# Norms of a two-layer trunk: the reciprocal root by a bit pattern and Newton steps on GpSimd in place of ScalarE's square root

## The chip, the cores and the metric

The kernel runs on one core of a Trainium2 chip. The metric is device time in microseconds (us) of one execution. Before the change three runs gave a median of 1860.58 us (1860.45 to 1862.76). The engines are named as in the profile: PE is TensorE (PEld its weight loads), DVE is VectorE, ACT is ScalarE, POOL is GpSimd, SP is SyncE, which issues most of the transfers.

## The reference, cut to what matters

A trunk of two layers on 512 tokens of width 1024. Each layer has a SwiGLU part, a mixer and another SwiGLU part, each behind a root-mean-square norm; a last norm follows. The mixer has eight forgetting-attention heads and four differential heads, whose outputs are normed once more, head by head ("norm of the diff heads").

```python
def _rmsnorm(x, gain):
    y = x32 * lax.rsqrt(jnp.mean(x32 * x32, axis=-1, keepdims=True) + NORM_EPS)
    return (y * gain).astype(x.dtype)
...
x = x + 1/2 * SwiGLU_1(RMSNorm(x))
x = x + W_out [FoX_heads(h) ; Diff_heads(h)],  h = RMSNorm(x)
x = x + 1/2 * SwiGLU_2(RMSNorm(x))
...
lam = exp(sum(lq1 * lk1)) - exp(sum(lq2 * lk2)) + lambda_init
o_d = _rmsnorm(o_d, subln) * (1.0 - lambda_init)
```

## The kernel before, in words

The tokens lie in four blocks of 128 (tiles `xs`), and every float32 operand of a large product is split in two parts, a rounded high part and the rest (low part), so that a product is three matmuls. For the mixer `prep_plain` turns a pair of 128-wide slices of x (k pair `kp`) with TensorE into a PSUM bank, scales it by the norm's gain and writes the operand tile `XA<kp>`: the high half by ScalarE (`act.activation`), the low half by VectorE (`scalar_tensor_tensor`). The root of the norm is not in these operands. It is applied to the results: the projections that follow (`proj`) start on the raw operands, and the root comes in as a row of 512 factors.

That row is made so. `half_squares` sums the squares on ScalarE into `s2`; `rms` adds the two halves (VectorE), scales, takes the square root on ScalarE, the reciprocal on VectorE, one Newton step (`refine`, four VectorE instructions) and the negative. All of it lies in the small tile `nst`, 128 partitions by 4 values. `diag` multiplies the unit matrix by the root of each of the four blocks (`dg`: two blocks on VectorE, two on ScalarE), and `finish_norm` multiplies `dg` by ones on TensorE, which spreads the row over the partitions; ScalarE copies it out as `rb`, and the rope tables are scaled by it. `finish_norm` is called in the middle of the second half of the first projection. It also makes `exl`, the two exponentials of the lambda, from `ls`.

The mixer's order of units is: first projection, then the values of the diff heads, then the rest of the projections between the heads' softmax. A head's softmax is a reduction on VectorE (`ISA` in the trace), exp on ScalarE, a reciprocal on VectorE and a scaling; TensorE turns the probabilities, ScalarE and VectorE split them (`pair`), and TensorE multiplies them with the values (`vd`, `vf`). When the last diff head is through, `stats` starts `diff_norm`: four rows of mean squares (`vv`) go by SP to HBM and come back as a tile `nd` of 64 partitions by 32 values; square root, reciprocal and `refine` follow, and the roots go by SP to HBM (`ms_d`) and come back spread over the partitions, one tile `rbd` for each head. VectorE multiplies each head with it (`ou`), and ScalarE and VectorE split the product (`y`) for the output projection.

ScalarE keeps its functions in tables. Where a square root stands between other functions, an `ACT_TABLE_LOAD` stands ahead of it and another ahead of the next exp or silu.

Each engine works its instructions off in one fixed queue. The order in these queues is set when the kernel is built, by a scheduler that estimates when each instruction can start; code that is written later may so stand earlier in a queue. `tc.issue_after(norm["root"].ins)` is a constraint on that scheduler: the exp of the lambda may not be queued ahead of the norm's square root.

Of the kernel before, what the change touches and what calls it, by code (L numbers as in the profile page):

```python
# [8 lines left out]
F32 = mybir.dt.float32  # L9
F32R = mybir.dt.float32r  # L10
BF16 = mybir.dt.bfloat16
AF = mybir.ActivationFunctionType
ALU = mybir.AluOpType
AX = mybir.AxisListType
# [38 lines left out]
def trunk(ctx, tc, xT, x, gains, gain_row, w_gu, w_dn, w_in, w_ff, w_out, fbias, lams, subln, consts, rope, out):  # L53
# [238 lines left out]
    def refine(y, v, t):  # L292
# [3 lines left out]
        dve.tensor_scalar(out=t, in0=t, scalar1=-0.5, scalar2=1.5, op0=ALU.mult, op1=ALU.add)  # L296
        dve.tensor_tensor(out=y, in0=y, in1=t, op=ALU.mult)

    norm = {}

    def squares(half):
# [13 lines left out]
            act.activation(out=sq, in_=xs[t][:, c * S:(c + 1) * S], func=AF.Square,  # L315
                           accum_out=norm["s2"][:, c, t:t + 1])

    def rms(ss=None):

        st = sm.tile([P, 4, NB], F32, tag="nst", name="nst", bufs=2)  # L320
        v, t, rc, nr = [st[:, i] for i in range(4)]
        if "s2" in norm:
            s2, ss = norm.pop("s2"), v
            dve.tensor_tensor(out=v, in0=s2[:, 0], in1=s2[:, 1], op=ALU.add)
        dve.tensor_scalar(out=v, in0=norm.pop("ss") if ss is None else ss, scalar1=1.0 / D, scalar2=EPS,
                          op0=ALU.mult, op1=ALU.add)
        norm["root"] = act.activation(out=rc, in_=v, func=AF.Sqrt)
        dve.reciprocal(out=rc, in_=rc)
        refine(rc, v, t)
        dve.tensor_scalar(out=nr, in0=rc, scalar1=-1.0, scalar2=None, op0=ALU.mult)  # L330
        norm["rc"], norm["nr"] = rc, nr

    def turn_x(half, kp, tag=None):
# [261 lines left out]
    def mixer(l, n_next, mid):  # L595
# [48 lines left out]
        def finish_norm():  # L644
            p = psum("b")
            pe.matmul(p, rf(ones), nrm.pop("dg"), start=True, stop=True)
            rb = nrm["rb"] = bb[0]
            act.copy(out=rb, in_=p)
            for i in range(2):
                dve.tensor_tensor(out=rope_t[i], in0=rope_t[i], in1=rb, op=ALU.mult)  # L650
            exl = sm.tile([P, 2], F32, tag="exl", name="exl", bufs=1)

            with tc.issue_after(norm["root"].ins):
                act.activation(out=exl, in_=ls, func=AF.Exp)
            dve.tensor_scalar(out=nlam, in0=exl[:, 1:2], scalar1=exl[:, 0:1], scalar2=-lam_init,
                              op0=ALU.subtract, op1=ALU.add)

# [306 lines left out]
        def diff_norm():  # L964

            v_d = dram.tile([DIFF_H, S], F32, name="v_d")
            ms_d = dram.tile([DIFF_H, S], F32, name="ms_d")
            for h in range(DIFF_H):
                sp.dma_start(out=v_d[h:h + 1, :], in_=vv[32 * h:32 * h + 1, :])
            nd = t_tile([64, 3, 32], F32, "nd")  # L970
            v, y, t = nd[:, 0], nd[:, 1], nd[:, 2]
            sp.dma_start(out=v, in_=v_d.rearrange("h (a b) -> (h a) b", b=32))
            act.activation(out=y, in_=v, func=AF.Sqrt)
            dve.reciprocal(out=y, in_=y)
            refine(y, v, t)
            sp.dma_start(out=ms_d.rearrange("h (a b) -> (h a) b", b=32), in_=y)

            def one(h):
                rbd = t_tile([P, S], F32, "rbd")
                sp.dma_start(out=rbd, in_=ms_d[h:h + 1, :].partition_broadcast(P))  # L980
                u = t_tile([P, S], F32, "ou")
                dve.scalar_tensor_tensor(out=u, in0=ov[h], scalar=sub_s, in1=rbd, op0=ALU.mult, op1=ALU.mult)
                split_o(4 + h, u)
            for h in range(DIFF_H):
                later.append(lambda h=h: one(h))
# [226 lines left out]
        for kp in (2, 3):  # L1212
            prep(1, kp, held.pop(0))

    def sums():
        half_squares((0, 1), 1)
        rms()


    xf = home("y0", [P, KP, 2, S], F32, "xin")  # L1220
# [111 lines left out]
    for l in range(DEPTH):  # L1332
# [6 lines left out]

        def mid():  # L1340
            rest_of(plain_)
            sums()
        mixer(l, n + 1, mid)
        pieces = {0: [lambda: [forms_(1, kp, None) for kp in (0, 1)]],
                  1: [lambda: [forms_(1, kp, None) for kp in (2, 3)], lambda: squares(1), rms]}
# [100 lines left out]
```

## Time and profile before

| | |
|---|---|
| median of 3 runs | 1860.58 us (1860.45 to 1862.76) |
| profiled execution | 1860.16 us, of which the span of the trace is 1858.2 us |
| granted TensorE clock | 0.998 |
| PE busy | 1829.4 us, 98% |
| VectorE busy | 1610.3 us, 87% |
| ScalarE busy | 1137.7 us, 61% |
| GpSimd busy | 128.2 us, 7%, in 154 instructions |
| bytes | 303.81 MB, mean 164 GB/s |

The span runs from the first to the last recorded instruction. In a row of a timeline the first number is the start, the second the duration, both in us; then engine, line, operation, and tiles as out<-in; in brackets stands the idle time ahead of it on its engine and what ended it. The mixer of layer 0 begins at about 350 us, that of layer 1 at about 1268 us.

### The profile page before, as it was taken

How to read it: one execution, taken by the hardware profiler on the slowest of the kernel's cores; microseconds unless marked ns; L12 is line 12 of the kernel's file. 1: busy time of each engine (PE TensorE's matmuls, PEld its weight loads, DVE VectorE, ACT ScalarE, POOL GpSimd, SP SyncE). 2: the span in 40 equal slices, each digit the busy share in tenths (PEclk: the TensorE clock that was granted, in tenths of full speed). 3: DMA queues.
4: the chain of work that ended last, by engine and by line, in shares of the span. 5: the costliest groups of instructions: out<-in, count | busy, mean ns of one | idle time of the engine just before them, and what ended most of it. 6: DMA issues, size and time to landing. Idle time of an engine off the chain costs nothing.

```text
span 1858.2 us, 24541 instructions
## 1 busy us (share of the span) xinstructions
PE 1829.4 (98%) x8702; PEld 1492.4 (80%) x8702; DVE 1610.3 (87%) x2531; ACT 1137.7 (61%) x1819; POOL 128.2 (7%) x154
## 2 busy tenths in 40 slices
PE   9999999999999999999999999999999999999997
PEld 5888888777878889888878988887777788888885
DVE  7898899888686999898998989997787869898998
ACT  7555555557795755565575556545677957455564
POOL 2010000000000100100000000000000000000101
PEclk9999999999999999999999999999999999999999
DMA  9786655243336775777557667543333467756742
GB/s 313 206 229 185 188 141 153 91 125 112 105 115 170 204 204 149 197 204 201 139 167 211 171 160 212 157 128 108 110 112 109 134 167 193 224 132 192 216 116 88
DMA packets 95531, 303.81 MB, mean 164 GB/s; under 512 B 12568, under 2 KB 15128, under 8 KB 95408
## 3 DMA queue, kind: packets, MB, share of 16 engines
q1 hardware_dynamic: 74816, 232.15, 36.9%
q0 software_dynamic: 19296, 68.17, 20.7%
q10 hardware_dynamic: 1296, 1.93, 0.3%
q8 instruction: 68, 1.11, 0.2%
q14 instruction: 55, 0.45, 0.1%
HBM read 287.45 MB, written 2.16 MB: 156 GB/s over the span
## 4 chain that ended last, share of the span: by engine, by line
PE 85%; DVE 8%; ACT 3%; DMA 2%; issue 1%; SPq 0%; DVEq 0%; ACTq 0%
PE ps_c L401 12%; PE ps_c L403 12%; PE ps_c L402 12%; PE ps L403 9%; PE ps L402 9%; PE ps L401 9%; PE ps_a L402 4%; PE ps_a L401 4%; PE ps_a L403 3%; DVE wg L84 2%; PE ps_t L497 2%; DVE x L526 1%; PE ps_g L1265 1%; PE ps_b L888 1%; PE ps_b L838 1%; PE ps_b L839 1%
## 5 line engine op out<-in xcount | busy, mean ns | idle before, releaser
L83 ACT CAST wg<-raw 128x1024 fp32r<-128x1024 f32 (+1 forms) x525 | 537.9, 1032 | 480.8 <-PE ps_c L403 173.0
L84 DVE TENSOR_TENSOR wg<-raw,wg 128x1024 fp32r<-128x1024 f32 (+1 forms) x525 | 621.2, 1194 | 101.1 <-ACT wg L83 96.5
L401 PE MATMUL ps_c<-wg,xf 128*128 128x512 f32 (+1 forms) x736 | 277.7, 378 | 1.7 <-ACT wg L83 1.6
L402 PE MATMUL ps_c<-wg,xf 128*128 128x512 f32 (+1 forms) x736 | 276.5, 376 | 1.4 <-DVE wg L84 1.4
L403 PE MATMUL ps_c<-wg,xf 128*128 128x512 f32 (+1 forms) x736 | 275.7, 375 | 0.0
L401 PE MATMUL ps<-wg,xf 128*128 128x512 f32 (+1 forms) x552 | 210.1, 381 | 0.0
L402 PE MATMUL ps<-wg,xf 128*128 128x512 f32 (+1 forms) x552 | 207.3, 376 | 0.9 <-DVE wg L84 0.9
L403 PE MATMUL ps<-wg,xf 128*128 128x512 f32 (+1 forms) x552 | 206.7, 376 | 0.0
L401 PEld LDWEIGHTS ps_c<-wg,xf 128*128 128x128 f32 x736 | 138.3, 188 | 28.6 <-ACT wg L83 2.5
L402 PEld LDWEIGHTS ps_c<-wg,xf 128*128 128x128 f32 x736 | 138.5, 188 | 27.2 <-DVE wg L84 2.2
L403 PEld LDWEIGHTS ps_c<-wg,xf 128*128 128x128 f32 x736 | 138.5, 188 | 25.0
L134 POOL DMA_DIRECT2D raw<-w_gu x86 | 74.6, 867 | 1129.7 <-DMA raw<-w_gu 628.0
L401 PE MATMUL ps_c<-wg,hf 128*128 128x512 f32 x352 | 138.5, 393 | 4.2 <-DVE x L526 4.0
L402 PE MATMUL ps_c<-wg,hf 128*128 128x512 f32 x352 | 137.4, 390 | 0.0
L403 PE MATMUL ps_c<-wg,hf 128*128 128x512 f32 x352 | 137.1, 390 | 0.0
L526 DVE SCALAR_TENSOR_TENSOR x<-ps_c,x 128x512 f32<-128x512 f32 x192 | 124.8, 687 | 1.3 <-PE ps_c L403 1.2
L402 PEld LDWEIGHTS ps<-wg,xf 128*128 128x128 f32 x552 | 104.0, 188 | 18.9 <-DVE wg L84 1.3
L403 PEld LDWEIGHTS ps<-wg,xf 128*128 128x128 f32 x552 | 103.8, 188 | 18.9
L401 PEld LDWEIGHTS ps<-wg,xf 128*128 128x128 f32 x552 | 104.0, 188 | 17.9 <-ACT xf L83 0.4
L401 PE MATMUL ps_a<-XA,wg 128*128 128x512 f32 x256 | 105.8, 414 | 2.2 <-ACT XA L355 1.8
L402 PE MATMUL ps<-wg,hf 128*128 128x512 f32 x264 | 103.1, 391 | 0.0
L401 PE MATMUL ps<-wg,hf 128*128 128x512 f32 x264 | 103.1, 390 | 0.0
(290 smaller groups left out, 3550.9 us busy)
## 6 DMA issues: line engine op xcount, KB each, us to landing
raw<-w_gu SPq DMA_DIRECT2D x218, 512.0 KB, 4.7
raw<-w_dn SPq DMA_DIRECT2D x100, 512.0 KB, 4.4
raw<-w_gu POOLq DMA_DIRECT2D x86, 512.0 KB, 6.8
raw<-w_in SPq DMA_DIRECT2D x48, 512.0 KB, 3.3
raw<-w_dn POOLq DMA_DIRECT2D x40, 512.0 KB, 5.9
kdup<-qk_t SPq DMA_DIRECT2D x64, 128.0 KB, 2.3
raw<-w_out SPq DMA_DIRECT2D x16, 512.0 KB, 3.2
raw<-w_dn SPq DMA_DIRECT2D x20, 256.0 KB, 3.8
```

The source lines that it names most:

```text
L83: act.copy(out=hi, in_=src)
L84: dve.tensor_tensor(out=lo, in0=src, in1=rf(hi), op=ALU.subtract)
L134: pool.dma_start(out=t, in_=where(two, h)[1], accum_op=ALU.add)
L401: pe.matmul(p, lh, rh, start=start, stop=False, skip_group_check=again)
L402: pe.matmul(p, lh, rl, start=False, stop=False, skip_group_check=again)
L403: pe.matmul(p, ll, rh, start=False, stop=stop, skip_group_check=again)
L497: pe.transpose(pj[j][:, e * 256 + p * P:e * 256 + (p + 1) * P], hs[j][p][:, o:o + P], ident)
L526: dve.scalar_tensor_tensor(out=xc, in0=src, scalar=scale, in1=xc, op0=ALU.mult, op1=ALU.add)
L838: pe.matmul(p[:, 0:w], lq, kk[m][:, 0, 0:w], start=True, stop=False)
L839: pe.matmul(p[:, 0:w], lq, kk[m][:, 1, 0:w], start=False, stop=not masked)
L888: pe.transpose(p[:, (qb - kb) * P:(qb - kb + 1) * P], probs[u][qb][:, kb * P:(kb + 1) * P], ident)
L1265: pe.matmul(pg[2 * half + j], gained(kp, e, half)[:, j * P:(j + 1) * P], w0[kp][:, e * S:(e + 1) * S], start=kp + e == 0, stop=kp == KP - ...
```

## The change

`inv_root` makes the reciprocal root without ScalarE: two VectorE instructions on the bits of v (shift right by one, subtract from a constant) give a first value; GpSimd makes h = -v/2 and three Newton steps of four instructions, y*y, times h, plus 1.5, times y. It is used for the norm that leads into the mixer (`rms(newton=True)`, where the negative goes to GpSimd too) and for the norm of the diff heads. The other norms keep the square root. The constraint on the exp of the lambda is gone.

```diff
+    def inv_root(y, v, t, h):
+
+        ti, yi = t.bitcast(I32), y.bitcast(I32)
+        dve.tensor_scalar(out=ti, in0=v.bitcast(I32), scalar1=1, scalar2=None, op0=ALU.logical_shift_right)
+        dve.tensor_scalar(out=yi, in0=ti, scalar1=-1.0, scalar2=float(0x5F3759DF), op0=ALU.mult, op1=ALU.add)
+        pool.tensor_scalar(out=h, in0=v, scalar1=-0.5, scalar2=None, op0=ALU.mult)
+        for _ in range(3):
+            pool.tensor_tensor(out=t, in0=y, in1=y, op=ALU.mult)
+            pool.tensor_tensor(out=t, in0=t, in1=h, op=ALU.mult)
+            pool.tensor_scalar(out=t, in0=t, scalar1=1.5, scalar2=None, op0=ALU.add)
+            pool.tensor_tensor(out=y, in0=y, in1=t, op=ALU.mult)
+
...
-    def rms(ss=None):
+    def rms(ss=None, newton=False):
...
-        norm["root"] = act.activation(out=rc, in_=v, func=AF.Sqrt)
-        dve.reciprocal(out=rc, in_=rc)
-        refine(rc, v, t)
-        dve.tensor_scalar(out=nr, in0=rc, scalar1=-1.0, scalar2=None, op0=ALU.mult)
+        if not newton:
+            act.activation(out=rc, in_=v, func=AF.Sqrt)
+            dve.reciprocal(out=rc, in_=rc)
+            refine(rc, v, t)
+        else:
+            inv_root(rc, v, t, nr)
+        (pool if newton else dve).tensor_scalar(out=nr, in0=rc, scalar1=-1.0, scalar2=None, op0=ALU.mult)
...
-
-            with tc.issue_after(norm["root"].ins):
-                act.activation(out=exl, in_=ls, func=AF.Exp)
+            act.activation(out=exl, in_=ls, func=AF.Exp)
...
-            nd = t_tile([64, 3, 32], F32, "nd")
-            v, y, t = nd[:, 0], nd[:, 1], nd[:, 2]
+            nd = t_tile([64, 4, 32], F32, "nd")
+            v, y, t, h_ = [nd[:, i] for i in range(4)]
...
-            act.activation(out=y, in_=v, func=AF.Sqrt)
-            dve.reciprocal(out=y, in_=y)
-            refine(y, v, t)
+            inv_root(y, v, t, h_)
...
         def mid():
             rest_of(plain_)
-            sums()
+            sums(True)
```

The scheduler answers with another order. In the rows below `waits` names the engine or DMA queue on which an instruction waits (Pool is GpSimd); each row is one instruction unless it ends with a count.

ScalarE, start of layer 0's mixer, before: the last pieces of XA, the norm's root, two `dg`, and the exp of the lambda.

```order
L355 ACTIVATE XA3_2805<-ps_t_2759,gains_sb_69 128x256 [waits DVE_49]
L355 ACTIVATE XA2_2800<-ps_t_2843,gains_sb_69 128x256 [waits DVE_49]
L355 ACTIVATE XA3_2805<-ps_t_2848,gains_sb_69 128x256 [waits PE_49]
L355 ACTIVATE XA3_2805<-ps_t_2848,gains_sb_69 128x256 [waits DVE_49]
L327 ACT_TABLE_LOAD
L327 ACTIVATE nst_2865<-nst_2865 128x4 [waits DVE_49]
L83 CAST wg_2892<-raw_2728 128x1024 [waits DMAHW6_49,PE_49]
L665 ACTIVATE dg_2887<-ident_88,nst_2865 128x128 [waits DVE_49]
L665 ACTIVATE dg_2887<-ident_88,nst_2865 128x128
L654 ACT_TABLE_LOAD
L654 ACTIVATE exl_2915<-ls_2820 128x2
```

The same place now:

```order
L371 ACTIVATE XA3_2805<-ps_t_2759,gains_sb_69 128x256 [waits DVE_49]
L668 ACT_TABLE_LOAD
L668 ACTIVATE exl_2924<-ls_2820 128x2 [waits DVE_49]
L371 ACTIVATE XA2_2800<-ps_t_2843,gains_sb_69 128x256 [waits DVE_49]
L371 ACTIVATE XA3_2805<-ps_t_2848,gains_sb_69 128x256 [waits PE_49]
L679 ACTIVATE dg_2896<-ident_88,nst_2865 128x128 [waits Pool_49]
L371 ACTIVATE XA3_2805<-ps_t_2848,gains_sb_69 128x256 [waits DVE_49]
L679 ACTIVATE dg_2896<-ident_88,nst_2865 128x128
L84 CAST wg_2901<-raw_2728 128x1024 [waits DMAHW6_49,PE_49]
```

The square root and its table load are gone, the exp and its table load stand ahead of three XA pieces, and the first `dg`, which waits for GpSimd, stands ahead of the last XA piece.

VectorE at the same place, now (before, both `dg` stood behind all XA pieces and behind the Newton step):

```order
L338 TENSOR_SCALAR nst_2865<-nst_2865 128x4 [waits DVE_49]
L303 TENSOR_SCALAR nst_2865<-nst_2865 128x4 [waits DVE_49]
L304 TENSOR_SCALAR nst_2865<-nst_2865 128x4 [waits DVE_49]
L669 TENSOR_SCALAR nlam_2822<-exl_2924 128x1 [waits Activation_49]
L372 SCALAR_TENSOR_TENSOR XA2_2800<-ps_t_2843,gains_sb_69,XA2_2800 128x256 [waits Activation_49]
L372 SCALAR_TENSOR_TENSOR XA3_2805<-ps_t_2848,gains_sb_69,XA3_2805 128x256 [waits Activation_49]
L677 TENSOR_SCALAR dg_2896<-ident_88,nst_2865 128x128 [waits Pool_49]
L677 TENSOR_SCALAR dg_2896<-ident_88,nst_2865 128x128
L372 SCALAR_TENSOR_TENSOR XA3_2805<-ps_t_2848,gains_sb_69,XA3_2805 128x256 [waits Activation_49]
L85 TENSOR_TENSOR wg_2901<-raw_2728,wg_2901 128x1024 [waits DMAHW6_49,Activation_49]
```

Both `dg` stand ahead of the low half of the last XA piece. In layer 1 the exp and its table load also stand ahead of the last three XA pieces on ScalarE, but all `dg` stay behind them.

VectorE, the norm of layer 0's diff heads, before:

```order
L874 ISA pg0_2811,st_4423<-ps_b_4424,rope_2619 128x512 [waits PE_49]
L874 ISA st_4423 128x1
L982 SCALAR_TENSOR_TENSOR ou_4304<-o0_2817,sub_s_2823,rbd_4302 128x512 [waits DMAHW7_49]
L84 TENSOR_TENSOR wg_4387<-raw_4128,wg_4387 128x1024 [waits DMAHW4_49,Activation_49]
L910 TENSOR_TENSOR y1_2814<-ou_4304,y1_2814 128x512 [waits Activation_49]
```

And now:

```order
L85 TENSOR_TENSOR wg_4405<-raw_4137,wg_4405 128x1024 [waits DMAHW4_49,Activation_49]
L891 RECIPROCAL st_4370<-st_4370 128x1 [waits Activation_49]
L912 TENSOR_TENSOR pair_4394<-ps_b_4390,pair_4394 128x384 [waits Activation_49]
L888 ISA pg0_2811,st_4414<-ps_b_4415,rope_2619 128x384 [waits PE_49]
L888 ISA st_4414 128x1
L994 SCALAR_TENSOR_TENSOR ou_4322<-o0_2817,sub_s_2823,rbd_4320 128x512 [waits DMAHW7_49]
L994 SCALAR_TENSOR_TENSOR ou_4353<-o0_2817,sub_s_2823,rbd_4351 128x512 [waits DMAHW0_49]
L994 SCALAR_TENSOR_TENSOR ou_4381<-o1_2818,sub_s_2823,rbd_4379 128x512 [waits DMAHW1_49,DVE_49]
L924 TENSOR_TENSOR y1_2814<-ou_4322,y1_2814 128x512 [waits Activation_49]
```

The split of a weight tile (`wg`) that stood behind the first `ou` stands ahead of it, and the softmax reduction of 512 columns that stood ahead of the first `ou` comes behind it.

More of the change, by code (lines that the diff above doesn't have):

```diff
@@ L11 @@
 BF16 = mybir.dt.bfloat16
+I32 = mybir.dt.int32
 AF = mybir.ActivationFunctionType
@@ L1213, in second_rest, with sums @@
             prep(1, kp, held.pop(0))
-    def sums():
+    def sums(newton=False):
         half_squares((0, 1), 1)
-        rms()
+        rms(newton=newton)
     xf = home("y0", [P, KP, 2, S], F32, "xin")
```

## The prediction, on record before the changed kernel ran

> **What bounds the kernel now.** I read the page first: its busy times and the chain that ended last.
>
> ```profile
> PE 1829.4 (98%) x8702; PEld 1492.4 (80%) x8702; DVE 1610.3 (87%) x2531; ACT 1137.7 (61%) x1819; POOL 128.2 (7%) x154
> PE 85%; DVE 8%; ACT 3%; DMA 2%; issue 1%; SPq 0%; DVEq 0%; ACTq 0%
> ```
>
> TensorE is busy for 98% of the span and carries 85% of the chain. A delay counts where TensorE has to wait for it; a saving on ScalarE counts only where TensorE waits for ScalarE. GpSimd is nearly empty. So the question is what the change does to the few places where TensorE waits. Next the groups by line, for what is removed, and then busy time by stretch, for the mixer's stage in which ScalarE matters:
>
> ```profile
> L327 ACT ACT_TABLE_LOAD x6 | 7.7, 1283 | 0.1
> L654 ACT ACT_TABLE_LOAD x2 | 2.6, 1283 | 0.0
> L973 ACT ACT_TABLE_LOAD x2 | 2.6, 1283 | 0.0
> L876 ACT ACT_TABLE_LOAD x2 | 2.6, 1283 | 0.0
> ...
> 520.00:560.00 40.00, 38.91 (x212) 30.06 (x212) 35.80 (x96) 39.51 (x97) 0.00 (x0) 1.00 0.37 113
> 1440.00:1480.00 40.00, 38.90 (x213) 30.01 (x212) 35.73 (x97) 39.51 (x97) 0.00 (x0) 1.00 0.38 113
> ```
>
> The columns of a stretch are its length, then TensorE, its weight loads, VectorE, ScalarE, GpSimd. From 520 to 560 us in layer 0, and from 1440 in layer 1, ScalarE is busy 39.51 of 40 us and TensorE idles 1.1. There alone can less ScalarE work shorten the run.
>
> **What the change removes.** Each layer loses three table loads: the root's (L327), the diff heads' root (L973) and the reload for exp behind it (L876). That is 6 x 1.283 = 7.7 us of ScalarE, plus two small square roots a layer. Where do they stand? First the start of layer 0's mixer, from the timelines of ScalarE, VectorE and TensorE:
>
> ```profile
> 350.41 0.47 ACT L355 ACTIVATE XA<-ps_t,gains_sb 128x256 fp32r<-128x256 f32 x1
> 351.33 0.98 ACT L355 ACTIVATE XA<-ps_t,gains_sb 128x256 fp32r<-128x256 f32 x2 [0.45 <-DVE XA L356]
> 352.87 0.47 ACT L355 ACTIVATE XA<-ps_t,gains_sb 128x256 fp32r<-128x256 f32 x1 [0.55 <-DVE XA L356]
> 353.36 1.28 ACT L327 ACT_TABLE_LOAD   x1
> 357.91 0.20 ACT L654 ACTIVATE exl<-ls 128x2 f32<-128x2 f32 x1
> ...
> 351.60 0.15 DVE L324 TENSOR_TENSOR nst<-ss 128x4 f32<-128x4 f32 x1
> 353.38 0.48 DVE L356 SCALAR_TENSOR_TENSOR XA<-ps_t,gains_sb,XA 128x256 fp32r<-128x256 f32 x1 [0.47 <-ACT XA L355]
> 355.10 0.16 DVE L294 TENSOR_TENSOR nst<-nst 128x4 f32<-128x4 f32 x1
> 355.30 0.16 DVE L295 TENSOR_TENSOR nst<-nst 128x4 f32<-128x4 f32 x1
> ...
> 352.34 0.39 PE L401 MATMUL ps_a<-XA,wg 128*128 128x512 f32 x1
> 353.70 0.61 PE L401 MATMUL ps_a<-XA,wg 128*128 128x512 f32 x2
> 357.11 1.02 PE L646 MATMUL ps_b<-dg,ones 128*128 128x512 f32 x2
> ```
>
> The root's table load starts at 353.36, when the last XA piece is already written (352.87 + 0.47), and TensorE takes that piece at 353.70 without a wait. The norm's result is first needed by the `dg` matmul at 357.11, which does not wait either. So these loads lie beside TensorE's work: nothing is gained here.
>
> The Trainium skill, "ScalarE: Activation LUTs", section "What ACT_TABLE_LOAD costs", adds about 1380 ns of drain to the 1283 ns of each switch. The trace shows the 1283, but only 0.02 us between the end of the ScalarE row ahead and the load at 353.36. By the page the removed ScalarE work would be 16.0 us; by the rows it is 7.7.
>
> **What it adds.** Each root is now two VectorE steps, then on GpSimd one product (h) and twelve instructions, each waiting for the one before it. VectorE's dependent steps start 0.20 us apart (355.10, 355.30) at 0.16 each, so a wait on one's own engine costs 0.04. For GpSimd the trace has no dependent chain, only single instructions:
>
> ```profile
> L258 POOL MEMSET zero<- 128x1 f32 x1 | 0.1, 98 | 0.0
> L281 POOL CAST ones<-stage 128x128 fp32r<-128x128 f32 x1 | 0.3, 283 | 0.0
> L641 POOL CAST tri<-tri_f 128x512 fp32r<-128x512 f32 x2 | 1.2, 618 | 9.0 <-DMA tri_f<-consts 9.0
> L1226 POOL TENSOR_SCALAR ngains<-gains_sb 128x56 f32<-128x56 f32 x1 | 0.4, 354 | 1.7 <-DMA gains_sb<-gains 1.7
> L1161 POOL TENSOR_TENSOR x<-x,gr 128x512 f32<-128x512 f32 x4 | 5.0, 1296 | 27.3 <-ACT sq L1136 27.3
> ```
>
> Lower end: a MEMSET of one column, 0.10 us a step. Upper end: the TENSOR_SCALAR whole, 0.354 + 0.04 = 0.39. Between: the two CASTs give (618 - 283)/384 = 0.87 ns an element and 0.17 us fixed; the TENSOR_SCALAR less 52 elements is 0.31. The product, like the CAST an ordinary small read and write, I put at 0.21 + 0.04 = 0.25, the sum step at 0.35; nine and three of them make 3.3 us, about **0.28 a step**. A chain of twelve is then 3.4 us, between 1.2 and 4.7.
>
> **Layer 0, start: +3.0 us.** The order has changed more than the diff. In the ScalarE queue the first `dg` (waiting for GpSimd) now stands ahead of the last XA3 piece; in VectorE's queue both `dg` stand ahead of that piece's low half. Whoever waits for GpSimd holds them up. The sums are at 351.60 as before; three VectorE steps at 0.20 put the first value y at 352.4. The chain ends at 352.4 + 3.4 = 355.8. `dg` and the high half take 0.05 + 0.35 + 0.47, so TensorE gets the piece at 356.7 in place of 353.70: **+3.0**. A floor lies under it: the exp's table load and exl (1.28 + 0.20) now stand ahead of XA2's second half, which moves from 351.33 to 352.4; it is written at 352.85 and its low half at 353.4, where TensorE wanted them from 352.34 on: +0.8. With steps of 0.10 the floor holds; with 0.39 it is 4.3.
>
> **Layer 1, start: +0.9 us.** Here both `dg` stand behind all XA pieces, but the exp's table load and exl went ahead of the last three:
>
> ```profile
> 1270.77 0.19 ACT L315 ACTIVATION_READ_ACCUMULATOR sq<-x 128x1 f32 x1
> 1271.28 0.47 ACT L355 ACTIVATE XA<-ps_t,gains_sb 128x256 fp32r<-128x256 f32 x1 [0.33 <-PE ps_t L339]
> ...
> 1272.42 0.48 DVE L356 SCALAR_TENSOR_TENSOR XA<-ps_t,gains_sb,XA 128x256 fp32r<-128x256 f32 x1
> ...
> 1272.50 0.44 PE L401 MATMUL ps_a<-XA,wg 128*128 128x512 f32 x1
> 1272.96 0.50 PE L402 MATMUL ps_a<-XA,wg 128*128 128x512 f32 x1
> 1277.63 1.02 PE L646 MATMUL ps_b<-dg,ones 128*128 128x512 f32 x2
> ```
>
> ScalarE has its squares behind it at 1270.96; load and exl end at 1272.46, XA3's first piece at 1272.9, XA2's second at 1273.3, its low half on VectorE at 1273.9. TensorE took that low half at 1272.96: **+0.9**. y stands behind it on VectorE, at 1274.05; the chain ends at 1277.4, both `dg` 0.75 later at 1278.2, and the `dg` matmul comes at 1277.63 + 0.9 = 1278.5: hidden by 0.3. At 0.39 a step it costs 0.9 more.
>
> **Diff heads: +1.3 us in each layer.** Here the root lies between two transfers through HBM:
>
> ```profile
> 499.89 0.17 DVE L877 RECIPROCAL st<-st 128x1 f32<-128x1 f32 x1 [0.88 <-ACT pg L876]
> 501.94 0.69 DVE L788 TENSOR_TENSOR qk<-kdup,qk 128x512 fp32r<-128x512 f32 x1
> 508.94 0.75 DVE L982 SCALAR_TENSOR_TENSOR ou<-o,sub_s,rbd 128x512 f32<-128x512 f32 x1 [0.49 <-DMA rbd<-ms_d]
> 509.61 1.22 DVE L84 TENSOR_TENSOR wg<-raw,wg 128x1024 fp32r<-128x1024 f32 x1
> ...
> 503.18 0.47 SPq L976 DMA_DIRECT2D ms_d<-nd  x1
> ...
> 518.51 0.39 PE L928 MATMUL ps_b<-pair,vf 128*128 128x256 f32 x1 [0.32 <-DVE pair L898]
> ```
>
> Before, the root was ready for SP at 503.18 and VectorE could start `ou` at 508.94, 5.76 later. Now VectorE makes y right behind the reciprocal at 499.89, by 500.5; twelve steps are 3.4, and 28 more elements a step at about 1.8 ns (between CAST and product) add 0.6. SP may issue at 504.5, 1.3 later, and `ou` follows at 510.3. VectorE, ScalarE's `y` casts and the next head's softmax stand behind `ou`; the wg split that used to stand behind it (1.22) goes ahead, but a softmax reduction of 512 columns goes behind. At 518.51 TensorE waits for VectorE with no slack, so I take the 1.3 as passed on. What speaks against it is the relief: two loads less are 2.6 us of ScalarE just ahead of its full stretch. I take it as spent waiting for `ou`. Bounds: at 0.10 a step the root comes a microsecond early and the relief is worth up to 2.8 (with the square root's 0.2) a layer; at 0.39 the loss is 2.6.
>
> **Sum.** 3.0 + 0.9 + 2 x 1.3 = 6.5. Against the profiled execution, 1860.16, that is 1866.7; the median of the runs is 0.4 above it, so I say **1867.0 us**.
>
> **Rivals.** *No change that can be told (within 0.2%, 3.7 us, about what a measurement here can tell).* GpSimd's step is VectorE's, 0.20: layer 0 loses 2.0, layer 1 0.9, the diff root is ready at 503.4 and its delay and the relief cancel: +2.9, 1863.5. For it: a CAST's fixed 0.17 with 0.04 is 0.21. Against: the only arithmetic row of small size took 354 ns.
>
> *Faster: ScalarE's relief decides.* Place: the stretch from 520, where ScalarE is full and TensorE short of it. Price: 2.8 us a layer. It decides once the diff root is ready by 503.18, that is below about 0.18 a step. With 0.10 the starts keep their floors, 0.8 + 0.9: 1.7 - 5.6 = -3.9, 1856.7. For it: the 39.51 of 40. Against: no GpSimd row that reads is below 283 ns.
>
> *Slower still: GpSimd is held up by VectorE.* If a GpSimd instruction cannot run beside a VectorE instruction on two tiles of SBUF, the diff chain stands still for two kdup rows of 0.69 and a wg row of 1.22: 2.6 a layer, 5.2 in all, 1872.3. The trace before has no pair of the two to judge by. That rule is the Trainium skill's: "SBUF — State Buffer", section "Who interferes with whom", says that a VectorE instruction with two SBUF inputs contends with a GpSimd instruction that reads SBUF, and that whichever starts first blocks the other. The slowest step of 0.39 alone comes out alike: 4.3 + 1.8 + 5.2 = 11.3, 1871.9.
>
> **Chances.** The forecast 0.50, still slower 0.15, no change 0.24, faster 0.11. So slower by over 0.2%: 0.65, within: 0.24, faster: 0.11. The range 1858 to 1875 leaves out the end of the fast rival and, above, both slow causes at once.
>
> **What would show it.** Six table loads fewer. GpSimd's nst rows 0.28 apart; below 0.18 or above 0.35 the sum is wrong. In layer 0 ScalarE waiting for GpSimd ahead of `dg`, then TensorE waiting some 2 to 3 us for XA with the last k block; if that row has no wait, the first term falls. In layer 1 a wait of under 1 us, from XA and not from `dg`. VectorE idle about 3 us ahead of the first `ou`, ended by the rbd transfer, and TensorE's wait for `pair` above 0.32; if instead that stage is no longer than before, the relief has won there.

## The result and the profile after

The changed kernel takes 1871.99 us (median of 4 runs, 1870.78 to 1874.62) against 1861.31 for the kernel before on the same chip: a ratio of 1.006, 95% interval 1.0047 to 1.0073. It is slower by about 10.7 us; the forecast was 1867.0, and its range to 1875 holds the result. The profiled execution took 1870.78, its span 1869.0.

The first lines of the page after:

```profile
PE 1832.3 (98%) x8702; PEld 1495.8 (80%) x8702; DVE 1607.5 (86%) x2517; ACT 1128.8 (60%) x1809; POOL 144.0 (8%) x208
PE 83%; DVE 10%; ACT 3%; DMA 2%; issue 1%; POOL 1%; SPq 0%; DVEq 0%; ACTq 0%; POOLq 0%
```

ScalarE lost 8.9 us of work and VectorE 2.8; GpSimd gained 15.8. TensorE's busy time rose by 2.9 us with the same 8702 matmuls, a first sign that its clock was lower somewhere.

**Where the time goes.** The matmuls are the same in both kernels, so the start of one TensorE instruction in both traces tells by how much the program has fallen behind at that place. From TensorE's timeline before, six such rows: the transposes ahead of the mixer, the sums of squares of the first diff head, a matmul of the second SwiGLU part's down projection; then for layer 1 a matmul of its first part's down projection, and the other two again.

```profile
345.46 0.44 PE L339 MATMUL ps_t<-ident,x 128*128 128x128 f32 x2 [1.10 <-DVE x L526]
433.94 0.42 PE L945 MATMUL ps_b<-pair,ones 128*32 128x512 f32 x1 [0.20 <-DVE pair L939]
915.38 0.47 PE L401 MATMUL ps_c<-wg,hf 128*128 128x512 f32 x1 [0.82 <-DVE x L526]
1251.62 0.47 PE L401 MATMUL ps_c<-wg,hf 128*128 128x512 f32 x1 [1.03 <-DVE x L526]
1354.76 0.42 PE L945 MATMUL ps_b<-pair,ones 128*32 128x512 f32 x1 [0.18 <-DVE pair L939]
1835.91 0.47 PE L401 MATMUL ps_c<-wg,hf 128*128 128x512 f32 x1 [0.82 <-DVE x L526]
```

The same rows after:

```profile
344.99 0.44 PE L355 MATMUL ps_t<-ident,x 128*128 128x128 f32 x2 [1.10 <-DVE x L542]
436.62 0.42 PE L959 MATMUL ps_b<-pair,ones 128*32 128x512 f32 x1 [0.20 <-DVE pair L953]
922.19 0.47 PE L417 MATMUL ps_c<-wg,hf 128*128 128x512 f32 x1 [0.82 <-DVE x L542]
1258.46 0.47 PE L417 MATMUL ps_c<-wg,hf 128*128 128x512 f32 x1 [1.07 <-DVE x L542]
1362.23 0.41 PE L959 MATMUL ps_b<-pair,ones 128*32 128x512 f32 x1 [0.19 <-DVE pair L953]
1846.90 0.47 PE L417 MATMUL ps_c<-wg,hf 128*128 128x512 f32 x1 [0.83 <-DVE x L542]
```

The lag is -0.47, 2.68, 6.81, 6.84, 7.47 and 10.99. So the start of layer 0's mixer costs 3.15 us, its heads 4.13, the stretch between the layers nothing, layer 1's start 0.63 and its heads 3.52: 11.4 in all, less the 0.47 by which this execution was ahead before it reached any changed instruction. The table below counts every kernel in this way; for the sums of squares it takes the matmul just ahead of the row shown (L944 before), which waits in no kernel.

**The start.** The waits of TensorE in layer 0 and layer 1 that have no like before, then what ScalarE and GpSimd do in layer 0:

```profile
352.34 0.50 PE L417 MATMUL ps_a<-XA,wg 128*128 128x512 f32 x1 [0.31 <-ACT XA L371]
356.19 0.73 PE L417 MATMUL ps_a<-XA,wg 128*128 128x512 f32 x2 [1.90 <-ACT XA L371]
1280.11 0.50 PE L417 MATMUL ps_a<-XA,wg 128*128 128x512 f32 x1 [0.58 <-ACT XA L371]
```

```profile
355.37 0.40 ACT L679 ACTIVATE dg<-ident,nst 128x128 f32<-128x128 f32 x1 [2.72 <-POOL nst L310]
355.68 0.45 ACT L371 ACTIVATE XA<-ps_t,gains_sb 128x256 fp32r<-128x256 f32 x1
...
351.98 0.20 POOL L307 TENSOR_TENSOR nst<-nst 128x4 f32<-128x4 f32 x1 [0.17 <-DVE nst L304]
355.14 0.20 POOL L310 TENSOR_TENSOR nst<-nst 128x4 f32<-128x4 f32 x1
```

The twelve GpSimd steps start between 351.98 and 355.14: eleven distances, 0.287 us each. ScalarE stands 2.72 us ahead of the `dg`, the last XA piece comes behind it at 355.68, and TensorE waits 1.90 us for that piece.

**The diff heads.** SP's queue, then VectorE's, in layer 0:

```profile
500.74 0.55 SPq L986 DMA_DIRECT2D nd<-v_d  x1
503.30 0.54 SPq L102 DMA_DIRECT2D raw<-w_out  x1
508.60 0.47 SPq L988 DMA_DIRECT2D ms_d<-nd  x1
510.29 1.28 SPq L992 DMA_DIRECT2D rbd<-ms_d  x3
...
513.62 0.75 DVE L994 SCALAR_TENSOR_TENSOR ou<-o,sub_s,rbd 128x512 f32<-128x512 f32 x1 [2.96 <-DMA rbd<-ms_d]
514.64 0.75 DVE L994 SCALAR_TENSOR_TENSOR ou<-o,sub_s,rbd 128x512 f32<-128x512 f32 x1 [0.27 <-DMA rbd<-ms_d]
516.16 0.75 DVE L994 SCALAR_TENSOR_TENSOR ou<-o,sub_s,rbd 128x512 f32<-128x512 f32 x1 [0.77 <-DMA rbd<-ms_d]
516.83 1.89 DVE L924 TENSOR_TENSOR y<-ou,y 128x512 fp32r<-128x512 f32 x3
518.63 0.68 DVE L972 TENSOR_TENSOR pg<-ps_b,fot 64x512 f32<-64x512 f32 x1
```

VectorE waits 2.96, 0.27 and 0.77 us for the rows of roots, does three `y`, and only then the fox heads' sum (`pg` from `fot`). The same place before:

```profile
497.48 0.55 SPq L972 DMA_DIRECT2D nd<-v_d  x1
505.67 1.28 SPq L980 DMA_DIRECT2D rbd<-ms_d  x3
...
511.35 1.41 DVE L982 SCALAR_TENSOR_TENSOR ou<-o,sub_s,rbd 128x512 f32<-128x512 f32 x2
512.67 0.68 DVE L958 TENSOR_TENSOR pg<-ps_b,fot 64x512 f32<-64x512 f32 x1
```

With the `ou` at 508.94 three of them stood ahead of the sum before too, but only one `y`. Counted from the load of `nd`, the first `ou` comes 1.42 us later than before (12.88 against 11.46) and the sum 2.70 (17.89 against 15.19). TensorE's two longest waits in the program end with this sum, one in each layer, and behind each the granted clock is low. TensorE's rows, then busy time by stretch, where the clock is the third number from the end:

```profile
519.46 0.42 PE L852 MATMUL ps_b<-qk 128*128 128x256 f32 x1 [3.67 <-DVE pg L972]
1444.32 0.36 PE L852 MATMUL ps_b<-qk 128*128 128x256 f32 x1 [3.63 <-DVE pg L972]
```

```profile
520.00:524.00 4.00, 4.00 (x14) 3.21 (x14) 3.90 (x9) 2.56 (x5) 0.00 (x0) 0.62 0.00 0
1444.00:1448.00 4.00, 3.68 (x11) 2.99 (x12) 3.91 (x9) 2.38 (x4) 0.00 (x0) 0.58 0.00 0
```

At 0.62 and 0.58 the two stretches lose some 1.5 us each (0.38 x 4.00 and 0.42 x 3.68). No stretch of the kernel before is below 1.00 there.

### The profile page after: what moved, and what is told of

Read it like the earlier page. It is cut to its first block, busy times and chain, and to the rows that moved or that the text cites. A ratio compares the mean times of both kernels' runs of the same rounds, so it can differ in the third digit from the quotient of the medians.

```text
span 1869.0 us, 24595 instructions
## 1 busy us (share of the span) xinstructions
PE 1832.3 (98%) x8702; PEld 1495.8 (80%) x8702; DVE 1607.5 (86%) x2517; ACT 1128.8 (60%) x1809; POOL 144.0 (8%) x208
## 3 DMA queue, kind: packets, MB, share of 16 engines
q10 hardware_dynamic: 1296, 1.93, 0.3%
HBM read 287.45 MB, written 2.16 MB: 155 GB/s over the span
## 4 chain that ended last, share of the span: by engine, by line
PE 83%; DVE 10%; ACT 3%; DMA 2%; issue 1%; POOL 1%; SPq 0%; DVEq 0%; ACTq 0%; POOLq 0%
PE ps_c L417 11%; PE ps_c L419 11%; PE ps_c L418 11%; PE ps L418 9%; PE ps L419 9%; PE ps L417 9%; PE ps_a L417 4%; PE ps_a L418 4%; PE ps_a L419 3%; DVE wg L85 3%; PE ps_t L513 2%; DVE x L542 2%; PE ps_b L902 1%; PE ps_g L1277 1%; ACT wg L84 1%
```

## The experiments

Three questions: do the places add, and what in each of them costs the time; is it the length of GpSimd's chain, the order that came with it, or GpSimd itself; and is there a version that beats both kernels. All ratios are to the kernel before on the same chip. The last four columns are the lag in us that each place adds in one profiled execution, counted as above against the one profiled execution of before. That one took 1860.16, less than the medians of the same kernel beside the others (1861.21 to 1862.53), so the columns show less gain than the medians. The stretch between the layers adds 0.9 us more in start_kept and slack2, at most 0.4 elsewhere.

| kernel | us | ratio (95%) | start 0 | heads 0 | start 1 | heads 1 |
|---|---|---|---|---|---|---|
| the change | 1871.99 | 1.006 (1.0047 to 1.0073) | 3.2 | 4.1 | 0.6 | 3.5 |
| mix_only | 1866.79 | 1.0021 (1.0011 to 1.003) | 3.2 | 1.0 | 0.5 | 0.0 |
| start_kept | 1870.90 | 1.0049 (1.0033 to 1.0064) | 1.3 | 5.5 | 0.5 | 3.3 |
| dg_kept | 1870.76 | 1.0045 (1.0028 to 1.0062) | 1.3 | 4.8 | 0.5 | 3.9 |
| slack2 | 1868.86 | 1.0035 (1.0022 to 1.0048) | 3.5 | 2.1 | 0.8 | 2.7 |
| steps2 | 1869.82 | 1.0047 (1.0033 to 1.0061) | 3.1 | 2.2 | 0.6 | 3.6 |
| steps1 | 1865.00 | 1.0022 (1.0012 to 1.0031) | 3.1 | 0.9 | 0.8 | -0.8 |
| diff_dve | 1857.75 | 0.9981 (0.9972 to 0.9991) | 1.1 | -1.2 | -0.3 | -1.7 |
| on_dve | 1859.63 | 0.9985 (0.9976 to 0.9994) | 1.1 | -0.1 | 0.6 | -1.8 |
| kept_slack3 | 1861.53 | 1.0003 (0.9994 to 1.0012) | 1.7 | -1.4 | 0.4 | 0.0 |
| diff_dve_slack3 | 1856.38 | 0.9977 (0.9968 to 0.9985) | 1.0 | -2.1 | -0.3 | -2.0 |
| before_slack3 | 1859.05 | 0.9982 (0.9973 to 0.9990) | 0.0 | -0.7 | -0.1 | -0.7 |
| onein | 1869.12 | 1.0037 (1.0023 to 1.0050) | 4.2 | 0.7 | 0.4 | 5.1 |

### The mixer's norm alone

```diff
...
-            inv_root(y, v, t, h_)
+            act.activation(out=y, in_=v, func=AF.Sqrt)
+            dve.reciprocal(out=y, in_=y)
+            refine(y, v, t)
```

> The root by Newton steps for the mixer's norm alone; the norm of the diff heads keeps ScalarE's root. Theory: the costs are separate and add. Counted by the start of the same TensorE rows in the two traces, the starts cost 3.15 us in layer 0 and 0.6 in layer 1, the diff heads 4.1 and 3.5. So this kernel loses 3.8 us against before (about 1865.1), with TensorE's wait of about 1.9 us ahead of the last k block in layer 0, no wait above 1 us at the diff heads and no stretch of 4 us with a granted clock below 0.9. Rival: the loss is one of the whole run (a lower clock or slower transfers because GpSimd works more): then some of the 10.7 us is lost here too beyond the 3.8.

mix_only took 1866.79, 4.3 us above the 1862.53 of the kernel before beside it; the starts cost 3.2 and 0.5, TensorE's wait ahead of the last k block is 1.91 us, no wait at the heads is above 0.89, and no stretch has a lower clock. The places add, and nothing is lost over the whole run that they do not account for. Layer 0's heads lose 1.0 us here although their code is the old one, a side effect of the shifted start that I did not follow further.

### What at the start costs the time

```diff
-                    dve.tensor_scalar(out=db, in0=ident, scalar1=r, scalar2=None, op0=ALU.mult)
+                    with tc.issue_after(norm["lo"].ins):
+                        dve.tensor_scalar(out=db, in0=ident, scalar1=r, scalar2=None, op0=ALU.mult)
...
-                    act.mul(out=db, in_=ident, mul=r)
+                    with tc.issue_after(norm["hi"].ins):
+                        norm["dg"] = act.mul(out=db, in_=ident, mul=r)
...
-            act.activation(out=exl, in_=ls, func=AF.Exp)
+            with tc.issue_after(norm["dg"].ins):
+                act.activation(out=exl, in_=ls, func=AF.Exp)
```

`lo` and `hi` are the last XA pieces on VectorE and ScalarE. start_kept has all three edits, dg_kept the first two.

> The change as it is, with constraints on the queues at the mixer's start: both dg stay behind the last XA piece on ScalarE and VectorE, and the exp of the lambda with its table load stays behind dg. The Newton chain on GpSimd is untouched. Theory: what cost time at the start is not the chain but what stood behind those who wait for it; the chain ends at about 355.4 us and dg is wanted at 356.6, so it is hidden. The start then costs 0 to 0.5 us a layer and the time is 3.3 to 3.8 us below the changed kernel's, about 1868.4. Rival: the chain itself is too slow and TensorE waits at the dg matmul: then less than 1.5 us comes back.

> The change with one of the two constraints alone: both dg stay behind the last XA piece, but the exp of the lambda and its table load stay ahead of three XA pieces, as in the change. Theory: the two causes add, and the second is the floor of the prediction, 0.8 us in layer 0 and 0.6 in layer 1; the first (waiting for GpSimd with an XA piece behind) is the rest, 2.3 us. So 2.3 us come back against the change (about 1869.7), and TensorE keeps a wait of 0.3 to 0.8 us for XA in layer 0. Rival: the exp's table load is the larger part: then under 1 us comes back.

Both kernels bring the start of layer 0 from 3.2 to 1.3 us. Of the two waits for XA dg_kept keeps only the 0.31 us, as the theory has it, and start_kept none. So the `dg` ahead of the last XA piece cost 1.8 us. What is left in dg_kept has the exp's table load ahead of it, but taking that away too (start_kept) gave no more, since another wait came in its place.

```profile
357.36 1.13 PE L663 MATMUL ps_b<-dg,ones 128*128 128x512 f32 x2 [0.27 <-ACT dg L683]
```

In start_kept VectorE does the XA pieces ahead of the scale of the squares, the chain starts at 353.22 instead of 351.98 (0.28 of this is the two traces' offset), ends at 356.58, and TensorE waits for `dg`. The theory that the chain hides altogether was short by this; the chain and the pieces compete for the same start. In both kernels little of it shows in the run's time (1870.90 and 1870.76, where 1868.4 and 1869.7 were expected), because layer 0's heads came out worse (5.5 and 4.8 us, with the granted clock down to 0.50 behind the wait there). So the 1.8 us is read from one profile of each kernel.

### The sum behind the roots: slack2

```diff
+            later.extend([lambda: None] * 2)
             for h in range(DIFF_H):
                 later.append(lambda h=h: one(h))
```

> The change as it is, but each of the four products of the diff heads with the root's row (ou) is handed to the program two steps of the heads' loop later, so that in VectorE's queue the sum of the fox heads' halves (pg from fot) stands ahead of all of them instead of behind three ou and three y. The Newton chain is as long as before. Theory: TensorE's wait of 3.7 us is for that sum, which sat behind instructions that wait for rbd; with it out of the way the wait goes, and with it the stretch of 4 us at a granted clock of about 0.6. 3 to 4 us a layer come back, about 1865. Rival: what is late is the chain, and whatever needs the diff heads' outputs passes the delay on: TensorE then still waits over 2 us, somewhere else, and the time stays above 1869.

The 3.67 us wait and the lower clock are gone, but only 2 us of layer 0's 4.1 and 0.8 of layer 1's 3.5 came back, and 1868.86 lies between the theory's 1865 and the rival's 1869: TensorE now waits twice for a `pair`. Its two waits, then the rows of ScalarE and VectorE that stand ahead of these pairs:

```profile
512.66 0.45 PE L941 MATMUL ps_b<-pair,vf 128*128 128x384 f32 x1 [1.56 <-ACT pair L911]
516.10 0.45 PE L942 MATMUL ps_b<-pair,vf 128*128 128x384 f32 x1 [1.24 <-DVE pair L912]
...
511.02 0.58 ACT L971 COPY fot<-ps_b 64x512 f32<-64x512 f32 x1 [1.97 <-DMA ms_d<-nd]
514.82 0.75 DVE L994 SCALAR_TENSOR_TENSOR ou<-o,sub_s,rbd 128x512 f32<-128x512 f32 x1 [1.94 <-DMA rbd<-ms_d]
```

The second is as the theory would have it, one place further on: a `pair` stands behind the first `ou`. The first is new. Small work tiles are handed out in turn from six places, and with `ou` handed over later the `fot` tile got the place of `nd`, so ScalarE waits for the write of the roots to leave it, with the cast of `pair` behind it. No other kernel has this wait. So it is not this one sum: whatever stands behind an instruction that waits for the roots is late with it.

### A shorter chain

```diff
-        for _ in range(3):
+        for _ in range(steps):
...
-            inv_root(y, v, t, h_)
+            inv_root(y, v, t, h_, 2)
```

This is steps2; steps1 has 1 in place of 2. `steps` is a new argument of `inv_root`, 3 where none is given, so the mixer's norm keeps three steps.

> The change with two Newton steps instead of three in the norm of the diff heads (the third, which refines the root, is left out); the order of VectorE's queue at the heads is the same. A step without a neighbour on VectorE took 1.26 us there, so SP's issue of the roots and the first ou come 1.26 us earlier. Theory: TensorE's wait shrinks by as much, from 3.7 to about 2.4 us, and because waits of up to 1.9 us were followed by no lower clock and those of 3.2 us and more by a stretch of about 4 us at 0.5 to 0.7, the stretch goes too, worth 1.5 us. Together 2.8 us a layer, 5.5 us below the change, about 1866.5. Rival: the lower clock does not hang on the wait: then 2.5 us in all come back, about 1869.5, and the stretch below 0.9 stays.

> The change with one Newton step in the norm of the diff heads (the second and third, which refine the root, are left out). From the load of nd to the issue of ms_d it took 5.70 us before, 7.86 with three steps, 6.53 with two. Theory: the loss at the heads hangs on the moment at which the roots leave; with one step they leave after about 5 us, before the old kernel's, so TensorE's wait for the fox heads' sum falls below 0.7 us, the lower clock goes, and the relief of ScalarE shows as in the kernel with the steps on VectorE (1.2 and 1.7 us a layer gained). With the start's 3.8 us, about 1862. Rival: that GpSimd works there is the cause, by its hold on VectorE or its semaphores: above 1866.

From the load of `nd` to the issue of `ms_d` it is 7.86 us with three steps, 6.53 with two, 4.71 with one (5.70 before). The heads follow, but not smoothly: 7.7 us for both layers with three, 5.8 with two, 0.1 with one. With two steps layer 0's wait fell to 2.04 us, further than the 2.4 foretold, yet the clock behind it was still low, so the theory that such a wait leaves the clock alone is wrong, and the run's time was the rival's. With one step 1865.00 lies between the theory's 1862 and the rival's 1866: layer 0 still has a wait of 1.93 us for the fox heads' sum, though its roots leave earlier than in the kernel before. SP's queue and VectorE's sum tell why, with the sum of diff_dve (the next section) in the last row:

```profile
503.31 0.54 SPq L102 DMA_DIRECT2D raw<-w_out  x1
505.45 0.47 SPq L988 DMA_DIRECT2D ms_d<-nd  x1
508.96 1.29 SPq L992 DMA_DIRECT2D rbd<-ms_d  x3
...
516.90 0.68 DVE L972 TENSOR_TENSOR pg<-ps_b,fot 64x512 f32<-64x512 f32 x1
...
514.85 0.68 DVE L969 TENSOR_TENSOR pg<-ps_b,fot 64x512 f32<-64x512 f32 x1
```

SP can issue `rbd` only 3.51 us after `ms_d`, against 1.69 in the change, so leaving early brings nothing: the sum starts 16.16 us after the load of `nd`, as in diff_dve (16.15), where TensorE waits 0.67 us for it. The other 1.26 us of the 1.93 is TensorE's own order. In steps1, as in the change, it is through with what stands ahead 15.06 us after that load (15.05 in the change), in diff_dve after 16.30, because the scheduler has put more of the other work in front there.

Why the `rbd` is late stays open. In layer 0 it comes 5.6 to 5.8 us after the last load of w_out in before, steps1 and diff_dve (503.31 to 508.96 here; 500.05 to 505.67 before; 501.26 to 507.01 in diff_dve), as if the small write lands only when that load of 512 KB is through; but in on_dve it is 6.5, in layer 1 of steps1 4.2, and no run moved the load.

### The same steps on VectorE

```diff
-        pool.tensor_scalar(out=h, in0=v, scalar1=-0.5, scalar2=None, op0=ALU.mult)
         for _ in range(3):
-            pool.tensor_tensor(out=t, in0=y, in1=y, op=ALU.mult)
-            pool.tensor_tensor(out=t, in0=t, in1=h, op=ALU.mult)
-            pool.tensor_scalar(out=t, in0=t, scalar1=1.5, scalar2=None, op0=ALU.add)
-            pool.tensor_tensor(out=y, in0=y, in1=t, op=ALU.mult)
+            dve.tensor_tensor(out=t, in0=y, in1=y, op=ALU.mult)
+            dve.scalar_tensor_tensor(out=t, in0=v, scalar=-0.5, in1=t, op0=ALU.mult, op1=ALU.mult)
+            dve.scalar_tensor_tensor(out=y, in0=t, scalar=1.5, in1=y, op0=ALU.add, op1=ALU.mult)
```

diff_dve uses this in the norm of the diff heads alone and leaves the mixer's norm as before; on_dve uses it in both.

> The kernel before with one edit: the norm of the diff heads takes its first value from bits and three Newton steps of three VectorE instructions each (no GpSimd, no square root on ScalarE, so four table loads fewer). The roots leave at about the same time as before (steps 0.2 us apart; one kdup row and one softmax reduction between them put the end some 0.5 us later). But three ou and three y now stand ahead of the fox heads' sum in VectorE's queue, as in the change. Theory: this order alone makes TensorE wait for that sum, about 2.5 us, with no stretch of lower clock; less the waits of 1.3 us that fall away behind it, 1.2 us a layer are lost, about 1865. Rival: the length of GpSimd's chain is the cause: then this kernel has no wait above 1 us there and gains the 1.1 us of idle a layer that ScalarE's load made, about 1860.

> The change with both norms' Newton steps on VectorE, three instructions a step, and nothing on GpSimd; ScalarE has lost the same table loads as in the change. Theory: only the engine of the steps separates the change from a gain. At the start the chain is 2.3 us in place of 3.4 and no dg stands ahead of an XA piece, so the exp's table load remains as the only cause, 1.3 us in layer 0 and 0.5 in layer 1; at the heads 1.2 and 1.7 us are gained: about 1860. Rival: VectorE, busy 87%, is made the bound by the extra instructions: above 1863.

diff_dve is faster than before, 1857.75, and my theory that the order alone costs 1.2 us a layer fell. Its queue also has three `ou` and three `y` ahead of the fox heads' sum, and the roots leave 5.74 us after the load of `nd`, as before; TensorE waits 0.67 us for the sum in layer 0 and not at all in layer 1. With the rows of roots on time this order costs little.

```profile
515.67 0.36 PE L849 MATMUL ps_b<-qk 128*128 128x256 f32 x1 [0.67 <-DVE pg L969]
```

The heads take 1.2 and 1.7 us less than before, near the 1.1 us of idle that the rival hoped for and well under the 2.8 us a layer at which the prediction priced ScalarE's relief. on_dve, the change with the steps moved to VectorE and each folded into three instructions, came out at 1859.63 where 1860 was expected: 12 us below the change, with the same six table loads removed. So what separates the change from a gain is where the steps run and how long they take, together with the queues that the scheduler makes of it. on_dve gains less than diff_dve in layer 0: its roots leave as early (5.75 us after the load of `nd`), but SP issues `rbd` 0.73 later counted from that load (9.04 against 8.31), and TensorE waits 1.50 us for the sum.

One thing in diff_dve was not foreseen. Its mixer's start is untouched and yet lies 1.1 us behind:

```profile
348.00:352.00 4.00, 4.00 (x14) 3.21 (x13) 3.85 (x12) 3.03 (x9) 0.00 (x0) 0.65 0.00 0
```

Here the granted clock is low behind waits of 1.09, 0.16 and 0.46 us within 3 us, waits that every kernel has at that place; on_dve and diff_dve_slack3 show the same, the others not. These three are the kernels with VectorE steps at the heads, but nothing that was changed there runs ahead of this place, so I have no cause for it.

### Later products

> The change with the two constraints at the mixer's start, and the ou of the diff heads handed over three steps of the heads' loop later, so that the fox heads' sum, a pair of 384 and a softmax reduction stand ahead of the first ou. Theory: nothing that TensorE wants soon stands behind an instruction that waits for the roots, so the wait of 3.7 us and the lower clock go and no others of over 1 us come in their place (with two steps a pair stood behind the first ou and cost 1.6 and 1.2 us). Left is the start, 1.3 and 0.5 us, and at the heads between -1 and +1 us a layer: 1863 to 1866. Rival: ScalarE and VectorE are full there, so that any shift costs: above 1867.

> The kernel diff_dve with its ou handed over three steps of the heads' loop later. Nothing is changed at the mixer's start. Theory: with neither a long chain nor the order against it, the relief of ScalarE (four table loads of 1.28 us fewer) can show: TensorE's waits between 500 and 560 us, 1.3 us before, shrink, and 0 to 1.2 us a layer are gained: 1860 to 1862.5, that is the same within what can be told, or just faster. Rival: moving ou later delays the output projection or the following heads: above 1864.

> The kernel before with one edit: the ou of the diff heads are handed over three steps of the heads' loop later. The square root and its table loads stay on ScalarE. Theory: what made the kernel with VectorE steps and later ou 4.8 us faster than before is mostly ScalarE's relief of two table loads and a root a layer; later ou alone are worth at most the 1.4 us by which the two VectorE kernels differ, so 1859.8 to 1861.5. Rival: the later ou are the gain and the relief is nothing: about 1856.5.

All three hand `ou` over three steps later (the edit of slack2 with 3 for 2): kept_slack3 to the change with start_kept's constraints, diff_dve_slack3 to diff_dve, before_slack3 to the kernel before. kept_slack3 takes 1861.53, below the 1863 to 1866 expected and the time of before: with three steps of room GpSimd's chain is hidden in layer 0 (1.4 us gained) and its delay shows in layer 1 as one wait of 1.62 us for a `pair`. diff_dve_slack3 is the fastest, 1856.38, better than I had expected and faster than both kernels. before_slack3 takes 1859.05, just below the bound that the theory gave: later `ou` are worth 3.1 us by themselves by the medians, 1.5 by the columns of the profile. By the single profiles the relief adds 1.4 and 1.3 us a layer on top (heads -2.1 and -2.0 against -0.7 and -0.7); the intervals of the two ratios overlap, so the medians alone do not tell it.

### Does VectorE hold GpSimd up: onein

```diff
-                dve.tensor_tensor(out=k_[:, 1], in0=dup, in1=rf(k_[:, 0]), op=ALU.subtract)
+                dve.tensor_scalar(out=k_[:, 1], in0=dup, scalar1=0.0, scalar2=None, op0=ALU.mult)
```

What raised the question are four rows of the changed kernel. GpSimd's steps on `nd`, two long ones and one of usual length, and the VectorE rows of the same moments:

```profile
504.69 0.72 POOL L310 TENSOR_TENSOR nd<-nd 64x32 f32<-64x32 f32 x1
506.14 0.77 POOL L309 TENSOR_SCALAR nd<-nd 64x32 f32<-64x32 f32 x1
507.96 0.28 POOL L309 TENSOR_SCALAR nd<-nd 64x32 f32<-64x32 f32 x1
...
504.61 0.69 DVE L802 TENSOR_TENSOR qk<-kdup,qk 128x512 fp32r<-128x512 f32 x1 [1.03 <-ACT qk L801]
506.07 0.69 DVE L802 TENSOR_TENSOR qk<-kdup,qk 128x512 fp32r<-128x512 f32 x1
507.65 0.69 DVE L912 TENSOR_TENSOR pair<-ps_b,pair 128x512 fp32r<-128x512 f32 x1
```

Each long step begins just behind a `kdup` subtraction with both inputs in SBUF and ends 0.1 to 0.15 us after it. The `pair` subtraction, as long but with one input in PSUM, holds nothing up.

> The change, but the low part of the diff and fox heads' keys (kdup) is made by a VectorE instruction with one SBUF input (kdup times zero) in place of the subtraction with two; the low part of the keys is so left out. In every kernel so far with Newton steps on GpSimd, just two of the steps in each layer took 0.71 to 0.78 us instead of 0.25 to 0.30, and both began beside a kdup subtraction of 0.69. Theory: that VectorE instruction with two SBUF inputs blocks GpSimd. Then no step is longer than 0.35 us here, the stretch from the load of nd to the issue of ms_d falls from 7.86 us to about 6.9, and TensorE's wait of 3.7 us by 1: 1868 to 1870. Rival: the two steps are long for another reason (the 64x32 tile, the transfers): then two long steps a layer stay and the time is the change's, 1872. If one long step of some 0.4 us stays beside a shorter kdup row, the one-input form blocks too.

One long step a layer is left, about as long as the shorter `kdup` row:

```profile
504.90 0.55 POOL L309 TENSOR_SCALAR nd<-nd 64x32 f32<-64x32 f32 x1
506.86 0.25 POOL L310 TENSOR_TENSOR nd<-nd 64x32 f32<-64x32 f32 x1
...
504.91 0.48 DVE L802 TENSOR_SCALAR qk<-kdup 128x512 fp32r<-128x512 f32 x1
506.77 0.69 DVE L912 TENSOR_TENSOR pair<-ps_b,pair 128x512 fp32r<-128x512 f32 x1
```

From the load of `nd` to `ms_d` it is 7.24 us against 7.86. So the long steps are the `kdup` rows' doing, and a VectorE row with a single SBUF input, this fast form of 0.48 us in place of 0.69, blocks too. The Trainium skill, "SBUF — State Buffer", section "Who interferes with whom", says both: a VectorE instruction with two SBUF inputs contends with a GpSimd instruction that reads SBUF, and so does a `tensor_scalar` that enters a two-port mode; whoever starts first blocks the other. The rows agree. The run's time says less than these rows: layer 0's heads improved to 0.7 us, with no low clock behind a wait of 2.87; layer 1's got worse, with a wait of 4.40, because the second `ou` waited 1.99 us for its `rbd`, which I cannot explain.

## Why the prediction was right or wrong

**Right: the bound, the cover of the table loads at the start, the step.** Six table loads are gone and nothing was gained at the starts by it. GpSimd's step was put at 0.28 us and is 0.287 on 128x4; on 64x32 an undisturbed Newton step of four takes 1.26 us, 0.32 an instruction, where 0.28 + 0.05 was used.

**Right: both starts.** Layer 0: +3.0 forecast, 3.15 measured, by the mechanism named; dg_kept shows 1.8 us of it to be the `dg` in the way, where the prediction had 2.2 above its floor. Layer 1: +0.9 forecast, 0.63 measured, with the wait for XA and none for `dg`.

**Wrong in size: the diff heads, +1.3 forecast, 4.13 and 3.52 measured.** This term carries the miss: 2.6 of the 6.5 forecast, 7.65 of the 11.4 measured. Its parts:

- The chain. The roots were to leave 1.3 us later. Counted from the load of `nd` (497.48 before), they left 2.16 later. The difference of 0.86 is the two steps held up by the `kdup` rows: 0.72 + 0.77 in place of 0.25 + 0.29, 0.95 us. The rival "GpSimd is held up by VectorE" named these rows, and onein shows them to be the cause; its third row, the wg split of 1.22, began at 508.43 when the last step was already running, and held nothing up, so its price of 2.6 a layer was too high.
- The transfer. `ou` was put at 510.3, 1.4 later than before, and from the load of `nd` it came 1.42 later in layer 0. That was luck: the path from `ms_d` to `rbd` gave 0.80 back there. In layer 1, where it gave nothing back, `ou` came 3.12 later (10.88 and 14.00 us).
- "I take the 1.3 as passed on." Here the step failed. TensorE's longest wait in the stage grew from 0.32 to 3.67 us, more than `ou` was late. It is a wait for the fox heads' sum, which came 2.70 us later: 1.42 with the first `ou`, and 1.28 from two more `y` and two further waits for a row of roots behind it, less the wg split that left this place. The prediction looked at what stood just behind the first `ou` before and now (wg, a softmax reduction) and not as far as the sum, nor at TensorE's own order. In diff_dve, with the same three `ou` and three `y` ahead of it, the sum comes 1.74 us earlier than in the change (16.15 against 17.89) and TensorE wants it 1.25 us later (16.30 against 15.05): its wait is 0.67. slack2 shows that it is not the sum alone.
- The relief was "taken as spent waiting". In diff_dve, where nothing waits long, the heads gain 1.2 and 1.7 us; in the change this is lost.
- The clock. Some 1.5 us a layer come from the low granted clock behind the long wait. The prediction had no term for it.

These parts are no exact sum: the wait's growth and the clock alone make 4.9 us in layer 0, 0.8 more than measured. TensorE's idle time summed over the whole place rose by 3.4 us and leaves the same gap, so it lies in the matmuls' own times or order; I have left that open.

**The rivals.** The total of "slower still" (1872.3) was met, and closer than the forecast's 1867.0, but by another sum: 0.95 us a layer of its mechanism, the rest waits and clock. "No change" fell with its condition, a step of 0.20 where 0.287 was measured. "Faster by ScalarE's relief" was right about what decides it, the moment at which the roots leave, but its price of 2.8 us a layer was too high: with the steps on VectorE it is 1.2 and 1.7.

## What to carry to other kernels

A chain of small dependent steps is priced by its latency, not its work: here moving nine or twelve tiny instructions between engines turned a gain of 2.5 us (on_dve) into a loss of 10.7, at the same relief of ScalarE. When an instruction in a full in-order queue waits longer, list everything that stands behind it until the bound engine's next need, not only the next row, and give such an instruction room by issuing it later; that alone (before_slack3) was worth 3 us. When TensorE is the bound, a wait of 3 us or more should be charged with a stretch of lower clock behind it; one near 2 us can have it too.

## What the runs showed of the hardware

TensorE's granted clock fell behind waits of different length. All eight waits of 3.1 us and more at the heads (the change twice, start_kept twice, dg_kept twice, steps2 and onein in layer 1) were followed by stretches of about 4 us (8 us in layer 0 of start_kept and dg_kept) with 0.50 to 0.71 as the lowest value; of the single waits between 1.5 and 2.9 us two were (steps2, 2.04, to 0.64; onein's start, 1.92, to 0.62) and most were not (onein, 2.87; steps1, 1.93; the change's start, 1.90); and clusters of shorter waits did it now and then: those at 345 us in three of fourteen profiles, 1.62 and 0.53 us at 955 us in four. One such stretch costs 1 to 2 us, the two longer ones 2.6. The Trainium skill, "TensorE: Matmul & The Clock Gate", section "HAM oscillation — how this bites in real kernels", asks for no idle gaps above about 3.4 us; seven of the eight long waits here (3.49 to 4.40 us) agree with it, and the one of 3.19 and the two near 2 us show that a shorter gap is not always safe.

GpSimd's product on 128x4 takes 0.20 us, less than its shortest row of before that reads (0.283), and the next dependent one starts 0.08 behind it, against 0.15 to 0.17 and about 0.04 on VectorE.
